# Attention blocks written to DRAM: GpSimd's DMA queue in place of SyncE's, for all head pairs but the last

## The chip, the cores and the metric

The kernel runs on one core of a Trainium2 chip. The metric is the device time of one execution in microseconds (us), from several executions of each kernel. A profiled execution gives, beside its own time, a trace of every engine: TensorE (PE, with its weight loads shown as PEld), VectorE (DVE), ScalarE (ACT), GpSimd (POOL) and SyncE (SP). DMAs are issued from the queues of SP, ACT and POOL; the issuing instructions stand in the trace as SPq, ACTq and, for GpSimd, as POOL rows named DMA_DIRECT2D.

## What is computed

One decoder layer for 512 tokens and 1024 channels in fp32, with two parallel attention branches of 8 heads of 64 channels each:

```
h = rms_norm(x, norm_w)
qa, ka, va, za, qb, kb, vb, zb, gl_a, gl_b = split(h @ w_in)
oa = moba_attention(rms_norm(qa), rms_norm(ka), va)       # softmax, with a bias by distance
ob = stick_breaking_attention(qb, kb, vb)                 # sigmoids and a running product along keys
ya = (oa * silu(za)) @ w_up_moba;  yb = (ob * silu(zb)) @ w_up_sb
x  = x + (sigmoid(gl_a + ba) * ya + sigmoid(gl_b + bb) * yb) @ w_out
```

With 512 tokens every past key is attended to in branch a, so each head has a lower-triangular matrix P of 512 x 512 weights, which is multiplied by its values. P is computed with queries on the partitions and is needed with keys on the partitions, so it has to be turned.

## The kernel before, in words

fp32 products run on TensorE as three passes over split operands: a high part `h` and a low part `l` (lines 234 to 236: l*h, h*l, h*h). Every weight block of 128 x 1024 comes in by one DMA from SP into a buffer `wr` (three buffers; line 160 in the stretch that matters here, line 179 elsewhere), ScalarE makes the high part `wh` (line 188), VectorE the low part `wl` (line 190). TensorE's first pass over a block needs only `wh`; its second needs `wl`. There are three buffers of each, so block n is loaded when `wl` of block n-3 is done, and split when TensorE is through with block n-3.

After the first products (up to about 145 us) comes a loop over eight pairs of heads, four of branch a (heads a0 to a7), then four of branch b (b0 to b7). For each pair:

- TensorE makes the scores of both heads (`scores`, line 513) into six PSUM banks, then multiplies the turned P of the pair two steps back by its values (`weighted`, line 608; `poa`, `pob`).
- VectorE and ScalarE make P row block by row block: in branch a (`softmax`, lines 533 to 541) with a bias tile `om` that SP loads by a DMA (`load_bias`, line 385; two buffers), in branch b (`stick`, lines 554 to 570) with scans on VectorE, in which `om` is written by ScalarE.
- `turn` (line 580) transposes P in blocks of 32 x 32 on VectorE into a tile `turned` (two buffers).
- `put` (line 587) writes `turned` to DRAM (`pd`) with four DMAs of 32 partitions, 160 KB each; `get` (line 594) reads it back in one DMA of 640 KB from ScalarE's queue into `pt`, with the 32 x 32 blocks in their turned places.
- Between these stand "fills": projections in chunks of 128 channels that have nothing to do with the pair (`gl`, `zb`, `kb`, and in later pairs `ya`, the product of branch a's output with its up-projection). They keep TensorE at work while P is made. The table `FILLS` says which fill stands where. `ya` of up:0 uses weight block 52, up:1 block 55.

GpSimd has little to do in the loop: at pairs 5, 6 and 7 it adds weight blocks in DRAM-to-SBUF DMAs for a later product (`sum_w`, lines 141 and 148). Each begins with a copy of one element that waits until the pair's `get` has landed, then loads a block, and then adds another onto it, once the first has landed.

The program's order on each engine is made by a scheduler that keeps data dependences and otherwise orders by its own estimates; the DMAs of one queue are issued in that order, and an instruction that waits holds what stands behind it on its engine or queue. ScalarE's queue too: a `get` that waits for its `put` holds ScalarE's next activation.

Of the kernel before, what the change touches and what calls it, by code (L numbers as in the profile page):

```python
# [32 lines left out]
PQ = 10 * 32  # L33
# [26 lines left out]
def hybrid_layer(ctx: ExitStack, tc: tile.TileContext, x, xT, w, rel, out):  # L60
    nc = tc.nc
# [232 lines left out]
    r = cp.tile([P, NT], F32, name="r")  # L294
# [288 lines left out]

    def put(br, h, turned):
        dr = dp.tile([P, 4 * PQ], F32, tag="pd", bufs=4, name=f"pd{br}{h}")
        for a in range(4):
            nc.sync.dma_start(bass.AP(tensor=dr.tensor, offset=dr.offset + a * PQ,
                                      ap=[[4 * PQ, 32], [32 * 4 * PQ, 4], [1, PQ]]),
                              turned[a * 32:(a + 1) * 32].rearrange("c q k r -> c q (k r)"))
        return dr  # L590

    def get(br, h, dr):
# [251 lines left out]
    for m, (br, p) in enumerate(PAIRS):  # L844
        raw[0] = br == "a"
        q, k = (qa, ka) if br == "a" else (qb, kb)
        sc = {h: {} for h in (2 * p, 2 * p + 1)}
        with tc.issue_after(end[0]):
            scores(br, p, q, k, sc)
        if m > 1:  # L850
            finish(m - 2, "pj")
        for b in range(2):
            h = 2 * p + b
            bias = load_bias(h) if br == "a" else None
            done[m, b] = put(br, h, turn(br, h, (softmax if br == "a" else stick)(h, sc[h], bias)))
            fill()
            if not b:
                done[m, 0] = get(*head(m, 0), done[m, 0])
        for b in range(2):
            if not b:  # L860
                done[m, 1] = get(*head(m, 1), done[m, 1])
            if (m, b) in SUMS:
                sum_w(SUMS[m, b], done[m, b])
            fill("pj" if (b or not fills[1]) and m < 7 else "s")
# [77 lines left out]
    for c in range(2):  # L942
        hi, lo = load_w()
        for t, ps, a, b in parts:
            for kk in range(2):
                k = 2 * c + kk
# [80 lines left out]
```

## Time and profile before

| | |
|---|---|
| three runs | 389.58, 388.64 and 423.43 us; median 389.58 |
| the profiled execution | 388.29 us, of which the span from first to last instruction is 386.5 |
| granted TensorE clock | 1.00 |
| busy share of the span | PE 98%, PEld 80%, DVE 74%, ACT 55%, POOL 21% |
| DMA | 86.38 MB, 223 GB/s |
| put's DMAs | 64 of 160 KB, all on SP; median 2.9 us (branch a) and 3.2 us (branch b) from issue to landing |

The one run of 423.43 us stands apart from the other two. The busy rows are of one execution; a wait is named by the engine and line that ended it last. In the timeline, a row's bracket is the idle time of the engine just before it.

### The profile page before, as it was taken

What the parts mean: (1) busy time and instruction counts of PE and PEld (TensorE: products, weight loads), DVE (VectorE), ACT (ScalarE), POOL (GpSimd) and SP (SyncE); (2) the same over time, 40 slices, a digit from 0 to 9 for tenths busy, and PEclk for the clock granted to TensorE, in tenths of its full rate; (3) what the DMA queues carried; (4) which work ended last, traced back from release to release, by engine and by line L of the source; (5) the groups of instructions that cost most, each with busy time, mean ns of one, the idle gap of its engine ahead of it and who ended that gap; (6) DMA issues with size and microseconds to landing.
All of it is one profiled execution on the core that took longest, in us unless ns stands there. A gap on an engine that the chain in (4) does not pass through costs nothing.

```text
span 386.5 us, 5481 instructions
## 1 busy us (share of the span) xinstructions
PE 379.2 (98%) x1935; PEld 308.3 (80%) x1935; DVE 284.5 (74%) x487; ACT 211.2 (55%) x367; POOL 80.0 (21%) x124
## 2 busy tenths in 40 slices
PE   8999999999999999999999999999999999999996
PEld 4888888888888998887878877776777877888885
DVE  4828999945777468972965399599939926999963
ACT  5685567338764447782853494554628213368540
POOL 3859959120210200000000000020101000420310
PEclk9999999999999999999999999999999999999999
DMA  7989799986864745569846826977697784599965
GB/s 264 342 332 336 198 234 274 283 277 238 209 173 100 190 124 187 146 204 335 242 110 207 308 69 213 303 181 226 190 332 257 159 331 132 173 254 294 177 155 175
DMA packets 36747, 86.38 MB, mean 223 GB/s; under 512 B 3944, under 2 KB 16744, under 8 KB 36720
## 3 DMA queue, kind: packets, MB, share of 16 engines
q1 hardware_dynamic: 27696, 52.72, 41.6%
q0 software_dynamic: 6576, 22.57, 24.6%
q10 hardware_dynamic: 2448, 10.75, 8.1%
q8 instruction: 15, 0.25, 0.2%
q14 instruction: 12, 0.10, 0.1%
HBM read 67.65 MB, written 14.70 MB: 213 GB/s over the span
## 4 chain that ended last, share of the span: by engine, by line
PE 82%; DVE 6%; DMA 5%; ACT 3%; issue 2%; SPq 2%; DVEq 0%
PE gl L234 6%; PE gl L235 6%; PE gl L236 6%; DMA pdb<-turnedb 3%; PE sa L513 2%; DMA wr<-in_w 2%; PE yb L234 2%; PE yb L235 2%; PE ka L235 2%; PE ka L234 2%; PE vx L235 2%; PE vx L234 2%; PE za L235 2%; PE za L234 2%; PE ka L236 2%; PE yb L236 2%
## 5 line engine op out<-in xcount | busy, mean ns | idle before, releaser
L190 DVE TENSOR_TENSOR wl<-wr,wh 128x1024 fp32r<-128x1024 f32 (+1 forms) x61 | 71.6, 1178 | 24.5 <-ACT wh L188 24.1
L188 ACT ACTIVATE wh<-wr 128x1024 fp32r<-128x1024 f32 (+1 forms) x61 | 63.2, 1036 | 46.2 <-DMA wr<-in_w 25.1
L234 PE MATMUL gl<-xl,wh 128*128 128x512 f32 x128 | 50.0, 391 | 0.0
L235 PE MATMUL gl<-xh,wl 128*128 128x512 f32 x128 | 49.8, 389 | 0.0
L236 PE MATMUL gl<-xh,wh 128*128 128x512 f32 x128 | 49.8, 389 | 0.0
L141 POOL COPY turn_of<-ptb 1x1 f32<-1x1 f32 x3 | 2.3, 758 | 148.9 <-DMA ptb<-pdb 148.9
L234 PEld LDWEIGHTS gl<-xl,wh 128*128 128x128 f32 x128 | 24.0, 188 | 5.2 <-issue 0.2
L236 PEld LDWEIGHTS gl<-xh,wh 128*128 128x128 f32 x128 | 24.0, 188 | 5.0
L235 PEld LDWEIGHTS gl<-xh,wl 128*128 128x128 f32 x128 | 24.0, 188 | 4.9
L635 ACT ACTIVATE gl<-gl,x 128x512 f32<-128x512 f32 x16 | 11.0, 685 | 20.8 <-PE gl L236 20.0
L533 DVE CUSTOM_DVE_ANT_0 pa<-sa,om 128x512 f32<-128x512 f32 (+3 forms) x32 | 13.9, 483 | 9.5 <-DMA om<-e_dr 6.8
L535 ACT ACTIVATE pa<-pa,m 128x512 f32<-128x512 f32 (+3 forms) x32 | 17.6, 552 | 5.0 <-DVE m L533 5.0
L558 DVE TENSOR_TENSOR_SCAN sx<-om,begin 128x512 f32<-128x512 f32 (+1 forms) x16 | 16.6, 1073 | 0.0
L580 DVE STREAM_TRANSPOSE turneda<-pa 128x384 f32<-128x384 f32 (+1 forms) x24 | 13.8, 605 | 2.6 <-ACT pa L539 2.4
L235 PE MATMUL ya<-oha,wl 128*128 128x512 f32 x32 | 12.8, 401 | 1.8 <-DVE wl L190 1.8
L580 DVE STREAM_TRANSPOSE turnedb<-pb 128x384 f32<-128x384 f32 (+1 forms) x24 | 13.6, 594 | 0.0
L234 PE MATMUL zb<-xl,wh 128*128 128x512 f32 x32 | 12.9, 404 | 0.0
L234 PE MATMUL kb<-xl,wh 128*128 128x512 f32 x32 | 12.7, 398 | 0.0
L234 PE MATMUL yb<-olb,wh 128*128 128x512 f32 x32 | 12.6, 393 | 0.0
L235 PE MATMUL zb<-xh,wl 128*128 128x512 f32 x32 | 12.5, 391 | 0.0
L236 PE MATMUL ya<-oha,wh 128*128 128x512 f32 x32 | 12.5, 390 | 0.0
L235 PE MATMUL yb<-ohb,wl 128*128 128x512 f32 x32 | 12.5, 390 | 0.0
(430 smaller groups left out, 1066.1 us busy)
## 6 DMA issues: line engine op xcount, KB each, us to landing
wr<-in_w SPq DMA_DIRECT2D x57, 512.0 KB, 5.5
pda<-turneda SPq DMA_DIRECT2D x32, 160.0 KB, 2.9
pta<-pda ACTq DMA_DIRECT2D x8, 640.0 KB, 5.1
pdb<-turnedb SPq DMA_DIRECT2D x32, 160.0 KB, 3.2
ptb<-pdb ACTq DMA_DIRECT2D x8, 640.0 KB, 4.9
qT<-in_w POOLq DMA_DIRECT2D x6, 512.0 KB, 5.9
xn<-in_x SPq DMA_DIRECT2D x8, 256.0 KB, 5.9
om<-e_dr SPq DMA_DIRECT2D x8, 256.0 KB, 4.3
```

The costliest lines, as they stand in the source:

```text
L141: with tc.issue_after(G.tensor_copy(turn_of, done[:1, :1].bitcast(F32)).ins):
L188: high[c] = A.activation(hi[:, a:b], raw[:, a:b], AF.Copy).ins
L190: low[c] = V.tensor_tensor(lo[:, a:b], raw[:, a:b], hi[:, a:b].bitcast(F32), op=ALU.subtract).ins
L234: T.matmul(ps, aH, bL, start=start, stop=False, skip_group_check=on)
L235: T.matmul(ps, aL, bH, start=False, stop=False, skip_group_check=on)
L236: end[0] = T.matmul(ps, aH, bH, start=False, stop=stop, skip_group_check=on).ins
L513: T.matmul(ps[b][:, c:c + n], x[o, i * P:(i + 1) * P], y[o, :n], start=m == 0, stop=m == 2)
L533: V.tensor_tensor_reduce(rows[i], sc[i], bias[:, S - n:], scale=1.0, scalar=3e38, op0=ALU.add, op1=ALU.min, accum_out=m[:, 0, i:i + 1])
L535: A.activation(rows[i], rows[i], AF.Exp, bias=m[:, 0, i:i + 1], scale=-1.0, accum_out=m[:, 1, i:i + 1])
L558: V.tensor_tensor_scan(sx[:, n - 1::-1] if n == S else sx[:, :n][:, ::-1], om[:, S + 1 - n:][:, ::-1], begin[:, S - n:S][:, ::-1], 0.0, op ...
L580: V.transpose(turned[:, :, at:at + n, :].rearrange("p q j r -> p j q r"), rows[i].rearrange("p (j q c) -> p j q c", j=n, q=4))
L635: evicted.append(A.activation(g, ps, AF.Identity if raw[0] else AF.Sigmoid, bias=mb[:, i:i + 1]).ins)
```

## The change

`put` takes its queue by the head: the last pair of branch b (heads b6 and b7) stays on SP, every other head's four DMAs are issued from GpSimd. Fourteen heads, 56 DMAs, move. What they copy, from where and to where, is the same.

```
     def put(br, h, turned):
         dr = dp.tile([P, 4 * PQ], F32, tag="pd", bufs=4, name=f"pd{br}{h}")
+        queue = nc.sync if br == "b" and h > 5 else nc.gpsimd
         for a in range(4):
-            nc.sync.dma_start(bass.AP(tensor=dr.tensor, offset=dr.offset + a * PQ,
-                                      ap=[[4 * PQ, 32], [32 * 4 * PQ, 4], [1, PQ]]),
-                              turned[a * 32:(a + 1) * 32].rearrange("c q k r -> c q (k r)"))
+            queue.dma_start(bass.AP(tensor=dr.tensor, offset=dr.offset + a * PQ,
+                                    ap=[[4 * PQ, 32], [32 * 4 * PQ, 4], [1, PQ]]),
+                            turned[a * 32:(a + 1) * 32].rearrange("c q k r -> c q (k r)"))
         return dr
```

From line 587 on, lines of the changed kernel have a number one higher. The scheduler also orders the other engines anew. Three places:

**The queues.** SP from head a4 to head b1, before (`wr` are weight blocks by their number, `om` bias tiles, `pda4` the DRAM block of head a4; x4 is four DMAs):

```order
L160 DMA wr46_2022<-in_w 128x1024
L587 DMA pda4_1915<-turneda4_1911 32x4x320 x4
L587 DMA pda5_1978<-turneda5_1974 32x4x320 x4
L587 DMA pda6_2121<-turneda6_2117 32x4x320 x4
L160 DMA wr47_2130<-in_w 128x1024
L385 DMA om1_121<-e_dr_88 128x512
L160 DMA wr48_2199<-in_w 128x1024
L160 DMA wr49_2234<-in_w 128x1024
L160 DMA wr50_2341<-in_w 128x1024
L587 DMA pda7_2190<-turneda7_2186 32x4x320 x4
L587 DMA pdb0_2332<-turnedb0_2328 32x4x320 x4
L587 DMA pdb1_2395<-turnedb1_2391 32x4x320 x4
```

and in the changed kernel:

```order
L160 DMA wr46_2022<-in_w 128x1024
L385 DMA om0_120<-e_dr_88 128x512
L385 DMA om1_121<-e_dr_88 128x512
L160 DMA wr47_2130<-in_w 128x1024
L160 DMA wr48_2199<-in_w 128x1024
L160 DMA wr49_2234<-in_w 128x1024
L160 DMA wr50_2341<-in_w 128x1024
L160 DMA wr51_2404<-in_w 128x1024
L160 DMA wr52_2439<-in_w 128x1024
```

Before, the bias tile of head a7 (`om1`) stands behind twelve puts, and blocks 51 and 52 behind those of a7, b0 and b1; now SP has only loads here. The puts stand on GpSimd, among the weight sums, in the changed kernel:

```order
L588 DMA pdb4_2762<-turnedb4_2758 32x4x320
L141 COPY turn_of_90<-ptb3_2650 1x1
L148 DMA T1b_2690<-in_w 128x1024
L588 DMA pdb4_2762<-turnedb4_2758 32x4x320
L148 DMA T1b_2690<-in_w 128x1024
L588 DMA pdb4_2762<-turnedb4_2758 32x4x320 x2
L588 DMA pdb5_2825<-turnedb5_2821 32x4x320 x4
```

Half of b4's put, and all of b5's, are behind the second T1b DMA, which adds onto the first and waits for its landing.

**VectorE ahead of `ya` of up:0**, before (`sx` and `pb` are the scans and P of a head, here of b2; `wl52` is the low part that `ya` waits for):

```order
L190 TENSOR_TENSOR wl51_2436<-wr51_2404,wh51_2435 128x1024
L558 SCALAR_TENSOR_TENSOR sx23_2532<-om1_121,begin_108 128x512
L558 SCALAR_TENSOR_TENSOR sx22_2537<-om0_120,begin_108 128x384
L560 TENSOR_TENSOR pb23_2528<-pb23_2528,sx23_2532 128x512
L560 TENSOR_TENSOR pb22_2529<-pb22_2529,sx22_2537 128x384
L568 SCALAR_TENSOR_TENSOR sx21_2542<-om_short_116,begin_108 128x386
L580 STREAM_TRANSPOSE turnedb2_2545<-pb23_2528 128x4x4x32
L570 TENSOR_TENSOR pb21_2527<-pb21_2527,sx21_2542 128x384
L580 STREAM_TRANSPOSE turnedb2_2545<-pb22_2529 128x3x4x32
L580 STREAM_TRANSPOSE turnedb2_2545<-pb21_2527 128x3x4x32
L190 TENSOR_TENSOR wl52_2555<-wr52_2439,wh52_2554 128x1024
```

and in the changed kernel:

```order
L190 TENSOR_TENSOR wl51_2436<-wr51_2404,wh51_2435 128x1024
L422 SCALAR_TENSOR_TENSOR kb3l_2467<-kb3_2441,kb3h_2466 128x512
L190 TENSOR_TENSOR wl52_2555<-wr52_2439,wh52_2554 128x1024
L558 SCALAR_TENSOR_TENSOR sx23_2532<-om1_121,begin_108 128x512
L558 SCALAR_TENSOR_TENSOR sx22_2537<-om0_120,begin_108 128x384
```

`wl52` has moved from behind all of b2's work to ahead of it.

**The pair of heads b4 and b5.** `wl55`, which `ya` of up:1 waits for, stands before behind the last transpose of b5; in the changed kernel it stands in the middle of b4:

```order
L781 TENSOR_TENSOR gl0_637<-ya0_2658,gl0_637 128x512
L781 TENSOR_TENSOR gl1_701<-ya1_2659,gl1_701 128x512
L558 SCALAR_TENSOR_TENSOR sx43_2745<-om1_121,begin_108 128x512
L560 TENSOR_TENSOR pb43_2741<-pb43_2741,sx43_2745 128x512
L558 SCALAR_TENSOR_TENSOR sx42_2750<-om0_120,begin_108 128x384
L580 STREAM_TRANSPOSE turnedb4_2758<-pb43_2741 128x4x4x32
L560 TENSOR_TENSOR pb42_2742<-pb42_2742,sx42_2750 128x384
L190 TENSOR_TENSOR wl55_2768<-wr55_2656,wh55_2767 128x1024
```

On TensorE, the last third of the scores of b4 and b5 (`sb41`, `sb51`) takes other PSUM banks. Before:

```order
L513 MATMUL sb52_2702<-kb2h_2157,qb2h_2161 128x384
L513 MATMUL sb41_2709<-kb2l_2158,qb2h_2161 128x256 [waits Activation_49]
L513 MATMUL sb41_2709<-kb2h_2157,qb2l_2162 128x256
L513 MATMUL sb41_2709<-kb2h_2157,qb2h_2161 128x256
L513 MATMUL sb41_2709<-kb2l_2158,qb2h_2161 128x128
L513 MATMUL sb41_2709<-kb2h_2157,qb2l_2162 128x128
L513 MATMUL sb51_2710<-kb2l_2158,qb2h_2161 128x256 [waits Activation_49]
```

and in the changed kernel:

```order
L513 MATMUL sb52_2702<-kb2h_2157,qb2h_2161 128x384
L513 MATMUL sb41_2709<-kb2l_2158,qb2h_2161 128x256 [waits DVE_49]
L513 MATMUL sb51_2710<-kb2l_2158,qb2h_2161 128x256 [waits DVE_49]
L513 MATMUL sb41_2709<-kb2h_2157,qb2l_2162 128x256
L513 MATMUL sb51_2710<-kb2h_2157,qb2l_2162 128x256
L513 MATMUL sb41_2709<-kb2h_2157,qb2h_2161 128x256
```

They waited for ScalarE to have read the scores of the same pair; now they wait for VectorE to have read `ya0` and `ya1` (`gl0`, `gl1` in the fence before, which stand right behind `wl53` and `wl54`). On ScalarE, the `get`s of b4 and b5 both stand ahead of the first activation of b6 before; in the changed kernel only that of b4 does.

## The prediction, as it went on record

> **What bounds the kernel now.** I read the page's busy shares first, then the windows of the pair loop, then what TensorE waited for, and last the queues and engines behind those waits.
>
> ```profile
> PE 379.2 (98%) x1935; PEld 308.3 (80%) x1935; DVE 284.5 (74%) x487; ACT 211.2 (55%) x367; POOL 80.0 (21%) x124
> ```
>
> TensorE is busy for 379.2 of 386.5 us at a granted clock of 1.00, and the change takes nothing off it. So it can win at most the part of the 7.3 idle us that the moved DMAs cause. The windows (us of the window, then busy us of PE, PEld, DVE, ACT, POOL, with instruction counts) say where in the loop there is any:
>
> ```profile
> 145.00:220.00 75.00, 75.00 (x412) 60.39 (x413) 48.85 (x135) 45.14 (x98) 0.00 (x0) 1.00 0.69 217
> 220.00:325.00 105.00, 102.51 (x558) 79.41 (x555) 82.54 (x120) 54.62 (x100) 6.39 (x9) 1.00 0.71 218
> ```
>
> Branch a's pairs leave none. From b0 on it is 105.00 - 102.51 = 2.5 us. The rest of the 7.3 lies at the start and in the tail, which the puts don't touch. TensorE's own timeline has the 2.5 us in three places:
>
> ```profile
> 256.70 0.50 PE L235 MATMUL ya<-oha,wl 128*128 128x512 f32 x1 [0.51 <-DVE wl L190]
> 264.05 0.38 PE L513 MATMUL sb<-kb2l,qb2h 64*128 64x256 f32 x1 [0.64 <-ACT pb L555]
> 280.71 0.50 PE L235 MATMUL ya<-oha,wl 128*128 128x512 f32 x1 [1.34 <-DVE wl L190]
> ```
>
> 0.51 + 0.64 + 1.34 = 2.49 us, all of it. Twice `ya` waits for the low part of its weight block (52, then 55); once the scores of b4 wait for a PSUM bank. SP's queue shows why the weight blocks are late (start, length from the first issue to the end of the last, count):
>
> ```profile
> 190.93 17.95 SPq L587 DMA_DIRECT2D pda<-turneda  x12
> 208.98 0.66 SPq L160 DMA_DIRECT2D wr<-in_w  x1
> 209.68 0.69 SPq L385 DMA_DIRECT2D om<-e_dr  x1
> ...
> 232.80 10.14 SPq L587 DMA_DIRECT2D pdb<-turnedb  x8
> 243.04 6.96 SPq L160 DMA_DIRECT2D wr<-in_w  x4
> ...
> L587 SPq DMA_DIRECT2D pdb<-turnedb x32: 303/432/1332, 232.8 to 307.9; - x32
> ```
>
> An issue takes 0.43 us (median), so the eight DMAs from 232.80 are 3.5 us of issuing in a stretch of 10.14. The rest is SP standing still for `turned`, with blocks 51 to 54 behind it until 243.04. And the bias tile of a7 goes out at 209.68, after twelve puts:
>
> ```profile
> 191.29 0.28 DVE L533 CUSTOM_DVE_ANT_0 pa<-sa,om 128x128 f32<-128x128 f32 x1
> 198.28 0.50 PE L513 MATMUL sa<-ka3l,qa3h 64*128 64x512 f32 x2
> 216.61 0.69 DVE L533 CUSTOM_DVE_ANT_0 pa<-sa,om 128x512 f32<-128x512 f32 x1 [6.26 <-DMA om<-e_dr]
> 219.20 0.50 PE L513 MATMUL sb<-kb0l,qb0h 64*128 64x512 f32 x2
> 224.26 1.28 ACT L554 ACT_TABLE_LOAD   x1
> 226.18 1.22 DVE L558 TENSOR_TENSOR_SCAN sx<-om,begin 128x512 f32<-128x512 f32 x1
> ```
>
> a7's scores exist from 198.28, its P is begun at 216.61. That pushes ScalarE's work on a7 to 224, so b0, whose scores begin at 219.20, gets its first scan at 226.18. **Branch b starts about 6 us late** and VectorE stays behind.
>
> **Part by part: what SP loses.** 56 issues of 0.43 us and their standing still go. The loads then wait for their buffers alone, that is for `wl` three blocks back. Of issuing alone 56 x 0.43 = 24 us leave SP; SP is on no path by itself, so this counts nothing.
>
> *The bias tile of a7* goes out ahead of the puts, right after that of a6. Its buffer was last read for a5, in the row at 191.29, so it is there when a7's scores are, and a6 and a7 are done one behind the other. I take it that ScalarE is through with a7 and its table loaded by 219, and b0's first scan comes 0.5 to 1 us after 219.20: at about 220 instead of 226.18, 6 us earlier.
>
> *Block 52.* Its load waits for nothing after 220, its `wh` for TensorE to be through with block 49. That is a `kb`, which ends where the scores of b2 begin:
>
> ```profile
> 240.19 0.50 PE L513 MATMUL sb<-kb1l,qb1h 64*128 64x512 f32 x2
> 261.91 0.50 PE L513 MATMUL sb<-kb2l,qb2h 64*128 64x512 f32 x2
> ...
> L190 DVE TENSOR_TENSOR wl<-wr,wh 128x1024 fp32r<-128x1024 f32 x27 | 32.3, 1206 | 2.8 <-ACT wh L188 2.7
> L188 ACT ACTIVATE wh<-wr 128x1024 fp32r<-128x1024 f32 x26 | 27.9, 1074 | 23.3 <-DMA wr<-in_w 21.8 <-issue 1.4
> ...
> 249.56 2.06 DVE L558 TENSOR_TENSOR_SCAN sx<-om,begin 128x512 f32<-128x512 f32 x2
> 255.47 1.18 DVE L190 TENSOR_TENSOR wl<-wr,wh 128x1024 fp32r<-128x1024 f32 x1
> 279.47 1.18 DVE L190 TENSOR_TENSOR wl<-wr,wh 128x1024 fp32r<-128x1024 f32 x1
> ```
>
> The split of `kb`, one `wh` and one `wl` later, 240.2 + 0.6 + 1.07 + 1.21, is 243.1, in the new order ahead of b2; needed at 256.2. Before, it began at 255.47. Term: **-0.51 us**, with 13 us to spare.
>
> *Block 55* was split at 279.47, behind b5. In the new order it stands behind two scans, two products and one transpose of b4, about 4 of the 5.9 us that a head of branch b takes on VectorE (255.47 - 249.56). b4's scores begin at 261.91 or a little before, and ScalarE and VectorE start on them 1 to 1.5 later, so `wl55` is done by about 268; needed at 278. Term: **-1.34 us**, with 10 us to spare.
>
> *The scores of b4 and b5* now wait for VectorE to have read `ya0` and `ya1`. By the new order, from b2's first scan at about 243.1 VectorE has two heads (11.8), three short operations of `kb`, `oa` and `ola` (1.9) and one of `zb` (0.6), so it is through with b3 at 257.4 (263.07 before), and with `wl53` and `wl54` at 259.8. `ya1` ends on TensorE with the fill, at 261.4 less the 0.51; its reading takes 0.6 to 0.7. TensorE comes to `sb51` 1.3 us after that fill ends. So the wait is 0 in the best case. In the worst, if VectorE were no earlier than before (263.07 + 2.4 + 1.3 = 266.8 against 262.6), it is 4.2. I take 0.3, since the 6 us of the late start decide and their cause is in the rows. Term: **-0.64 + 0.3 us**.
>
> **What GpSimd takes on.** No row has a put from GpSimd. The nearest are its loads of 128 rows, since a put is 128 pieces too:
>
> ```profile
> L444 POOL DMA_DIRECT2D kaT<-kadr x4: 536/537/538, 82.0 to 84.8; - x4
> L121 POOL DMA_DIRECT2D vT3a<-in_w x1: 1242/1242/1242, 48.7 to 48.7; - x1
> DMA to landing us min/median/max: 3.6/7.8/12.0
> ...
> 277.01 0.55 POOL L148 DMA_DIRECT2D T1b<-in_w  x1
> 283.42 0.86 POOL L148 DMA_DIRECT2D T1b<-in_w  x1 [5.85 <-DMA T1b<-in_w]
> ```
>
> From 0.54 to 1.24 us each: a put is 2.2 to 5.0 us of issue against 1.7 on SP. I take 2.2, the plain case of the same count of pieces. Heads come every 6 us or more, so the queue keeps up at either end. Cost on the path: nothing, as P is used two pairs later, about 20 us. The cover is thinnest where the second T1b DMA waits for the first, 6.4 us from 277.01 to 283.42, with half of b4's put behind it. T1b starts when b3's `get` lands. That `get` stands behind the first activation of b5 in the new order, at about 268 to 269, so T1b starts at about 274. The second T1b goes out at 280.4, and b4's put behind it is issued by 282 and lands by 287, at which b4's `get` lets ScalarE go on to b6. How late may that be? The rows of before have the landing times of branch b's puts and of its `get`s, the start of b6 on ScalarE, the `get`s of b6 and b7, and the last `pob`:
>
> ```profile
> DMA to landing us min/median/max: 2.1/3.2/6.5
> ptb<-pdb ACTq DMA_DIRECT2D x8, 640.0 KB, 4.9
> ...
> 291.94 0.58 ACT L554 ACTIVATE om<-sb 128x512 f32<-128x512 f32 x1
> 306.97 6.33 ACTq L594 DMA_DIRECT2D ptb<-pdb  x2
> 318.21 3.03 PE L608 MATMUL pob<-ptb,vbs 128*64 128x128 f32 x28
> ```
>
> The second of the two `get`s ends at 313.3 and lands 4.9 later, 26.3 us after b6's start. TensorE needs it for the second half of a run of 40 products from 318.21 less the gain, that is at 318.3. So b6 may begin at 292.0; 287 leaves 5 us.
>
> **The sum.** 388.29 - 0.51 - 1.34 - 0.34 = **386.1 us** for a profiled execution. The runs of before that agree, 388.64 and 389.58, have a mean of 389.1, 0.8 above their profiled one (their median of three, 389.58, is 1.3 above). So I predict **386.9 us** for the runs.
>
> One rule speaks against any gain. The Trainium skill (DMA: Bandwidth & Descriptors, Issuing engines are not separate DMA queues) says that DMAs of all issuing engines run on the same 16 DMA engines, and that issuing from more of them saves only sequencer time, usually small. By it the sum is -24 us of SP's time off the path, thus 388.3. The 10.14 us row disagrees: there the loads stood behind what the puts waited for, not behind their issue.
>
> Another (SBUF — State Buffer, Summary: rules for kernel authors) advises SP or ACT for a DMA under VectorE work, since GpSimd's descriptors starve while VectorE is in a doubled mode. These rows say which operations could be meant:
>
> ```profile
> L541 DVE TENSOR_SCALAR pa<-pa,m 128x256 f32<-128x256 f32 x8 | 2.8, 354 | 0.2
> L541 DVE TENSOR_SCALAR pa<-pa,m 128x128 f32<-128x128 f32 x8 | 2.3, 282 | 0.0
> ```
>
> 128 more elements in 72 ns is nearly two per ns, and they run in branch a alone. By that rule a put of branch a is up to 0.6 us late, where TensorE has no idle time; the three terms lie in branch b. So it doesn't raise the second rival below, as it would if all of VectorE's work shut GpSimd out.
>
> **The rivals.** *No gain:* the loads wait for their buffers nearly as long, or for the same DMA engines (busy share 0.71 in the loop), and the waits of `ya` stay. For: the 23.3 us that ScalarE idled before `wh` are mostly put down to the load itself. Against: buffers 52 and 55 come free over 10 us before they are needed. Time: 388.3 + 0.8 = 389.1.
>
> *VectorE's reading of `ya` becomes the wait.* If the start of branch b is less than about 4 us earlier, `sb51` waits up to 4.2 us where 0.64 was lost: -0.51 - 1.34 - 0.64 + 4.2 = +1.7, or 390.8. It decides as soon as b3's last transpose on VectorE ends after 259.0.
>
> *GpSimd's queue runs late.* At 1.24 us a DMA and 12.0 us to the landing of T1b, the second T1b goes out at 287.2, it and half a put are issued by 291.0, and it lands 3.2 to 6.5 later (median and slowest of these on SP), at up to 297.5: 5.5 us past the 292.0, all of them a wait of TensorE at the last `pob`. -2.2 + 5.5 = +3.3, or 392.4. It decides when b4's put lands after 292.
>
> That the change doesn't do what it says I leave out: the order has every put but two off SP.
>
> **How the numbers follow.** The forecast (a gain of 1.5 to 2.5 us) has 0.62, no gain 0.16, VectorE's reading 0.12, GpSimd's queue 0.10. The likeliest's own range is 386.0 to 388.2. Low end of the range: all 2.5 us gone, and runs that lie no higher than the profiled one less 0.5, 385.3. High end: the first slower rival, 390.8; past it lies half of the second. A measurement of this kernel can tell about 2%, 7.8 us, from no change. Faster by that has 0.01, since TensorE's idle time in reach is 2.5 us; slower by that 0.04, for a queue that is later than both bounds; within it 0.95.
>
> **What would show it.** Right: `om` of a7 issued before 200 and no wait of VectorE for it; b0's first scan near 220; no wait of `ya` for `wl`; GpSimd's put DMAs near 0.54 us; PE busy in 220 to 325 but for some 0.3 us. Wrong: PE waiting for `gl` at the scores of b4 or b6, for a `ptb` at `pob`, or b4's put landing after 292. If GpSimd's DMAs take over 1.24 us each, or ScalarE stands at `get`s of branch a, the bounds above are too narrow.

## The result, and the profile after

The changed kernel is slower: median 391.1 us of 20 runs, beside 388.75 of the kernel before; ratio 1.0053, 95% interval 1.0033 to 1.0073. Four of the changed kernel's runs (395.5 to 396.05 us) and one of the kernel before (423.43) lie apart from the others, and the ratio leaves them out. The difference is within 2%, on the wrong side of the forecast of 386.9 and just past its range (385.3 to 390.8). The profiled execution took 391.13 us, span 389.3 (before 388.29 and 386.5).

The same two windows as before (us, then busy us of PE, PEld, DVE, ACT, POOL), and what TensorE waited for in the loop:

```profile
145.00:220.00 75.00, 75.00 (x413) 60.41 (x413) 52.09 (x143) 49.48 (x109) 17.69 (x32) 1.00 0.73 239
220.00:325.00 105.00, 100.44 (x548) 78.20 (x546) 79.52 (x111) 50.35 (x89) 18.31 (x33) 0.98 0.67 208
```
```profile
PE gl L234 <- DVE ob L614: 3.4, 1, 3.4
PE kb L234 <- DVE zb L623: 1.1, 1, 1.1
```

The three old waits (`ya` twice, the scores of b4) are gone. Two new ones stand in the loop, 3.4 and 1.1 us, and the granted clock, 1.00 before, is 0.98. TensorE's timeline at the larger one:

```profile
293.23 0.39 PE L236 MATMUL zb<-xh,wh 128*128 128x512 f32 x1
297.06 0.47 PE L234 MATMUL gl<-xl,wh 128*128 128x512 f32 x1 [3.44 <-DVE ob L614]
297.36 0.40 PE L235 MATMUL gl<-xh,wl 128*128 128x512 f32 x1
...
299.13 0.63 PE L235 MATMUL gl<-xh,wl 128*128 128x512 f32 x1
299.56 0.63 PE L236 MATMUL gl<-xh,wh 128*128 128x512 f32 x1
299.99 0.63 PE L234 MATMUL gl<-xl,wh 128*128 128x512 f32 x1
```
```profile
298.50:301.70 3.20, 3.20 (x9) 2.43 (x9) 3.20 (x5) 0.50 (x1) 0.02 (x1) 0.50 0.82 262
```

The wait is for a PSUM bank of `pj`, which VectorE frees by reading `pob1` into `ob1` (line 614). Behind it eight matmuls start 0.43 us apart instead of 0.23: the clock is 0.50 there, and 8 x 0.2 = 1.6 us more are lost. Backwards from it, GpSimd, ScalarE and VectorE:

```profile
273.61 0.55 POOL L588 DMA_DIRECT2D pdb<-turnedb  x1 [10.73 <-DVE turnedb L580]
...
274.38 0.56 POOL L148 DMA_DIRECT2D T1b<-in_w  x1
275.25 0.56 POOL L588 DMA_DIRECT2D pdb<-turnedb  x1 [0.32 <-issue]
278.99 0.91 POOL L148 DMA_DIRECT2D T1b<-in_w  x1 [3.19 <-DMA T1b<-in_w]
279.57 3.10 POOL L588 DMA_DIRECT2D pdb<-turnedb  x5
```
```profile
279.71 1.66 ACT L643 ACTIVATE gl<-gl 128x512 f32<-128x512 f32 x3
288.45 0.33 ACTq L595 DMA_DIRECT2D ptb<-pdb  x1
288.83 0.60 ACT L554 ACTIVATE om<-sb 128x512 f32<-128x512 f32 x1 [7.46 <-DMA pdb<-turnedb]
```
```profile
289.46 1.23 DVE L558 TENSOR_TENSOR_SCAN sx<-om,begin 128x512 f32<-128x512 f32 x1 [5.15 <-ACT om L554]
...
295.79 0.51 DVE L570 TENSOR_TENSOR pb<-pb,sx 128x384 f32<-128x384 f32 x1
296.23 0.68 DVE L614 TENSOR_TENSOR ob<-pob,zb 128x512 f32<-128x512 f32 x1
```

Half of b4's put stands behind the second T1b DMA, which waits for the first. The put goes out by about 280.7 and lands at 288.45, where b4's `get` leaves ScalarE; ScalarE has stood idle for 7.46 us by then, some 4 of them after b6's first scores were there. So b6's first scan is at 289.46, though b6's scores were begun at 283.51, and `ob1`, ready soon after 288, is read behind eight operations of b6 and one `wl`. Where TensorE stands along the loop (starts of the scores of b2, b4, b6 and of the last `pob`; before: 240.19, 261.91, 286.19, 318.21):

```profile
241.61 0.50 PE L513 MATMUL sb<-kb1l,qb1h 64*128 64x512 f32 x2
262.53 0.50 PE L513 MATMUL sb<-kb2l,qb2h 64*128 64x512 f32 x2
283.51 0.50 PE L513 MATMUL sb<-kb3l,qb3h 64*128 64x512 f32 x2
...
320.64 4.54 PE L609 MATMUL pob<-ptb,vbs 128*64 128x128 f32 x40
```

It is 2.7 us ahead at b6's scores and 2.4 behind at the last `pob`: 5.1 us lost in this one place, 3.6 from start to start and 1.6 of half rate.

### The profile page after: what moved, and what is told of

Same layout as the page of the kernel before. It is cut to its first block, busy times and chain, and to the rows that moved or that the text cites. A ratio compares the mean times of both kernels' runs of the same rounds, so it can differ in the third digit from the quotient of the medians.

```text
span 389.3 us, 5495 instructions
## 1 busy us (share of the span) xinstructions
PE 379.9 (98%) x1935; PEld 309.0 (79%) x1935; DVE 285.1 (73%) x487; ACT 211.1 (54%) x367; POOL 109.0 (28%) x180
## 4 chain that ended last, share of the span: by engine, by line
PE 84%; DVE 5%; issue 4%; DMA 3%; POOL 1%; ACT 1%; DVEq 0%; ACTq 0%; POOLq 0%
PE gl L234 7%; PE gl L236 7%; PE gl L235 7%; PE sa L513 2%; PE kb L234 2%; PE yb L234 2%; PE kb L236 2%; PE ka L235 2%; PE ka L236 2%; PE yb L236 2%; PE kb L235 2%; PE yb L235 2%; PE vx L236 2%; PE vx L235 2%; PE za L236 2%
## 5 line engine op out<-in xcount | busy, mean ns | idle before, releaser
L234 PE MATMUL gl<-xl,wh 128*128 128x512 f32 x128 | 50.8, 397 | 3.4 <-DVE ob L614 3.4
L588 POOL DMA_DIRECT2D pda<-turneda x32 | 17.7, 555 | 63.7 <-DVE m L536 42.5
L588 POOL DMA_DIRECT2D pdb<-turnedb x24 | 14.0, 660 | 39.6 <-DVE turnedb L580 35.6
L554 ACT ACTIVATE om<-sb 128x512 f32<-128x512 f32 (+1 forms) x16 | 8.9, 558 | 13.4 <-DMA pdb<-turnedb 7.5
L329 POOL TENSOR_SCALAR e_sb<-rb 8x1 f32<-8x1 f32 (+11 forms) x32 | 10.7, 362 | 6.5 <-DMA rb<-in_rel 6.5
```

The source lines that it names most:

```text
L234: T.matmul(ps, aH, bL, start=start, stop=False, skip_group_check=on)
L329: last["table"] = G.tensor_scalar(e_sb[:, m:m + n], rb[:, b:b + 1].to_broadcast([H, n]), -1.0, 1.0, op0=ALU.mult, op1=ALU.mult).ins
L588: queue.dma_start(bass.AP(tensor=dr.tensor, offset=dr.offset + a * PQ, ap=[[4 * PQ, 32], [32 * 4 * PQ, 4], [1, PQ]]), turned[a * 32:(a + 1 ...
```

## The experiments

Medians are of one group of runs on one chip beside the kernel before (388.6 to 388.9 in the four groups). "Half rate" counts the runs with a mean granted clock below 0.997; in a run without a trace the clock is all that is known, not what TensorE waited for.

**b4's and b5's puts back on SyncE.**
```
-        queue = nc.sync if br == "b" and h > 5 else nc.gpsimd
+        queue = nc.sync if br == "b" and h > 3 else nc.gpsimd
```


> Only the puts of b4 and b5 go back to SyncE; VectorE's order around `ob1` stays nearly as in the changed kernel (`ob1` behind b6's scans). Theory 1 (b4's put stands behind T1b's sum in GpSimd's queue, so its `get` holds ScalarE to 288.45, b6's scans start at 289.46 instead of about 285.0, and `ob1`, which stands seven operations behind the first of them, frees a bank of `pj` 3.4 us too late): b4's `get` goes out before 280, `ob1` is read by 291.5, no wait of `gl` (3.4 us gone), no half-rate stretch behind it (1.6 us gone, granted clock 1.00), the wait of `kb` of 1.1 us stays: 391.1 - 3.4 - 1.6 = 386.1, bounds 385.6 to 387.0. Theory 2 (VectorE's new order alone makes the wait, whenever the put lands): `gl` still waits at least 2 us, 389 or more. Theory 3 (GpSimd's puts cost by themselves, through the DMA engines, all along): 48 of 56 puts are still there, 390.5.

387.1 us, ratio 0.9941 (0.9919 to 0.9964), no wait of `gl`, half rate in none of 12 runs. Theory 1's step holds. Theories 2 and 3 fall: `ob1` still stands behind b6's scans, and 48 of 56 puts are still on GpSimd. The median is 1 us above the 386.1, mostly in the spread from 386.3 to 387.9.

**VectorE reads `pob1` first.**
```
+        last["po"] = V.tensor_tensor(dst, po..., z, op=ALU.mult).ins
-            with tc.issue_after(split_of[1]) if h % 2 == 0 and i == 3 else nullcontext():
+            with tc.issue_after(last["po"] if h == 6 else split_of[1]) if h % 2 == 0 and i == 3 else nullcontext():
```


> All of the changed kernel's puts stay on GpSimd; VectorE's reading of `pob1` is put ahead of b6's first scan. Theory 1: b4's `get` is as late as before (288.4), b6's first scan is at 289.5, but `ob1` is read at about 288 to 290, so the 3.4 us wait of `gl` and the 1.6 us of half rate are gone, 1.1 us of `kb` stay: 386.1, bounds 385.6 to 387.2. Theory 2 says the same here. Theory 3 (late puts cost by themselves, wherever VectorE reads): the wait moves to another place, `pob` or `ya`, and the time stays at 389 or more.

A miss for theory 1: 390.63 us, ratio 1.0039 (1.0012 to 1.0067), half rate in 9 of 12. The `gl` wait is gone and another has come. What TensorE waited for, and VectorE's timeline:

```profile
PE ya L235 <- DVE wl L190: 2.5, 1, 2.5
```
```profile
291.68 1.23 DVE L190 TENSOR_TENSOR wl<-wr,wh 128x1024 fp32r<-128x1024 f32 x1 [7.02 <-ACT wh L188]
292.82 0.68 DVE L614 TENSOR_TENSOR ob<-pob,zb 128x512 f32<-128x512 f32 x1
293.42 2.06 DVE L558 TENSOR_TENSOR_SCAN sx<-om,begin 128x512 f32<-128x512 f32 x2
...
306.39 2.31 DVE L190 TENSOR_TENSOR wl<-wr,wh 128x1024 fp32r<-128x1024 f32 x2
```

b4's `get` leaves ScalarE at 288.48 as in the changed kernel, so b6 is late all the same. Its first scan, 293.42, is where the kernel before had it (293.02), while TensorE comes over 2 us earlier; the next thing behind b7 on VectorE, `wl` of block 59, makes TensorE wait for what it had won. So the place of `ob1` only says where the late put is paid. I took that order for a part of the cause, and it isn't.

**The sum of T1b one pair later.**
```
-SUMS = {(4, 1): ("T1a",), (5, 1): ("T1b",), (6, 1): ("T2a",)}
+SUMS = {(4, 1): ("T1a",), (6, 1): ("T1b", "T2a")}
```


> All puts stay on GpSimd; the sum of T1b is made one pair later, together with T2a, so that no sum stands ahead of b4's put. Theory 1: b4's put lands by 279, no wait of `gl`, 386.1, bounds 385.6 to 387.5 (two sums at once at about 300 share the DMA engines with the last `get`s). Theory 2: `gl` waits 2 us or more, 389 or more. Theory 3: 390.5.

386.92 us, ratio 0.9944 (0.992 to 0.9968), half rate in none of 12: all puts on GpSimd, and a gain. The two sums at once cost 0.7 us at the last `pob`, which waited for its load.

**Only branch a's puts on GpSimd.**
```
+        queue = nc.sync if br == "b" else nc.gpsimd
```


> Only branch a's puts are on GpSimd, all of branch b's are on SyncE as before; VectorE's order is nearly that of the changed kernel, with `ob1` even further back, behind b7's first scan. Theory 1: the bias tile of a7 is early as in the changed kernel, so is b0's first scan (222.9), no sum stands ahead of a put, `ob1` is read by about 293, so `gl` waits 0 to 0.5 us, and the loads of blocks 52 and 55 stand ahead of the puts of their pairs, so `ya` does not wait: 386.3, bounds 385.6 to 387.5. Theory 2: the wait of `gl` is 3 us or more, 389.5. If the loads of the weights still stood behind branch b's puts, `ya` would wait up to 1.9 us again: 388.

385.48 us, ratio 0.9894 (0.9857 to 0.9932), 0.8 below theory 1's 386.3. One wait is left in the loop, `kb` for `zb`, 1.1 us.

**The same, and `zb0` earlier on VectorE.**
```
+        last["z"] = V.tensor_tensor(zr[br, p], ps, zr[br, p], op=ALU.mult).ins
+        with tc.issue_after(last["z"]) if h == 1 else nullcontext():
             V.tensor_tensor_scan(sx[:, :n][:, ::-1], short...
```


> The kernel with only branch a's puts on GpSimd (385.5 us), and VectorE's product of `zb0` put ahead of b1's last scan, so that the bank of `pj` for `kb3` comes free earlier. If the one wait left in its loop (`kb` for `zb`, 1.1 us at about 236) is VectorE's order alone: `zb0` is read at about 232.5 instead of 235.2, the wait is gone, nothing takes its place: 384.4, bounds 384.0 to 384.9. If VectorE is simply full there, `kb` no longer waits but b1 and b2 are later by as much and a `ya` waits instead: 385.5.

385.27 us, ratio 0.9913 (0.9893 to 0.9933): the wait falls from 1.1 to 0.4 (`zb0` is read at 234.60), but the runs lie between 384.6 and 386.3, and the two medians don't tell whether the time fell.

**b4's put alone, of branch b's, on GpSimd.**
```
+        queue = nc.gpsimd if br == "a" or h == 4 else nc.sync
```


> The kernel with only branch a's puts on GpSimd (385.5 us), and b4's put alone on GpSimd as well: four DMAs more, in the one place where they stand behind the sum of T1b. The theory after the first four runs (one late put, that of b4, holds ScalarE at its `get` to about 288.5 and with it b6 and b7 on VectorE; TensorE falls back to the timetable of before at whatever stands behind them, `gl` or `ya`): a wait of 2.5 to 3.5 us at 293 to 308, in part of the runs 1.7 us of half rate behind it: 388 without the half rate, 389.7 with it, median 389.3, bounds 387.8 to 390.5. If it takes many puts on GpSimd (traffic or descriptor work all along), four DMAs change nothing: 385.7.

A miss: 385.79 us, ratio 0.9913 (0.9893 to 0.9932). GpSimd's timeline, and ScalarE's:

```profile
273.83 0.55 POOL L148 DMA_DIRECT2D T1b<-in_w  x1 [0.48 <-ACT pb L555]
276.02 0.57 POOL L588 DMA_DIRECT2D pdb<-turnedb  x1 [1.64 <-DVE turnedb L580]
277.88 0.89 POOL L148 DMA_DIRECT2D T1b<-in_w  x1 [1.29 <-DMA T1b<-in_w]
278.48 1.99 POOL L588 DMA_DIRECT2D pdb<-turnedb  x3
```
```profile
284.73 0.33 ACTq L595 DMA_DIRECT2D ptb<-pdb  x1
285.89 0.60 ACT L554 ACTIVATE om<-sb 128x512 f32<-128x512 f32 x1 [3.14 <-PE sb L513]
```

The put is issued by 280.5, no sooner than in the changed kernel, yet lands 4.3 us later instead of 7.7, just as b6's scores arrive. One of its six runs took 391.73 at a clock of 0.991; what it waited for was not recorded.

**Only the bias tiles off SyncE** (the kernel before, all puts on SyncE).
```
     def load_bias(h):
-        nc.sync.dma_start(bt, ...
+        nc.gpsimd.dma_start(bt, ...
```


> The kernel before, all puts on SyncE, and only the bias tiles of a2 to a7 (six loads) go through GpSimd's queue. If the late bias tile of a7 behind the puts is what makes branch b late, and with it the weight blocks and the scores that TensorE waits for: b0's first scan at about 223 instead of 226.2, the waits of `ya` and `sb` gone but for some 0.5 us, 386.6, bounds 385.8 to 387.4. If the weight loads behind branch b's own puts are a cause of their own, the two waits of `ya` stay, 0.5 + 1.3: 388.3. If neither matters, 388.9.

386.74 us, ratio 0.9946 (0.9928 to 0.9964). The edit moves all eight bias loads, not six: those of a0 and a1 go out at 27.7 us, long before the loop, the other six from 153.0 to 185.8. b0's first scan is at 223.71, and the window of the loop has no idle time:

```profile
220.00:325.00 105.00, 105.00 (x579) 82.43 (x578) 81.79 (x113) 52.01 (x90) 6.29 (x9) 1.00 0.73 227
```

With branch b in time all three old waits are gone, and branch b's own puts ahead of the weight loads cost nothing. The time is near that of the kernels with 48 or 56 moved puts in which nothing waits for b4's (386.0 to 387.1), and above the 385.48 of the one with branch a's 32. Its profile has a wait of TensorE of 1.5 us near the start (`psR`), outside the loop, that the others don't have; what brings that on was not tested.

**Only branch b's puts on GpSimd.**
```
+        queue = nc.sync if br == "a" or h > 5 else nc.gpsimd
```


> Only branch b's puts (b0 to b5) are on GpSimd, branch a's on SyncE. Theory: a7's bias tile is late as in the kernel before, b0's first scan at about 226, and b4's put stands behind the sum of T1b and lands at 290 or later; the waits of `ya` for blocks 52 and 55 are gone (1.9 us), but b6 is late and `gl` or `ya` waits 3 us or more: 390, bounds 388.5 to 392.5. If taking branch b's puts off SyncE were a gain by itself, 387.0.

391.93 us, ratio 1.009 (1.0066 to 1.0113), half rate in all six. b0's first scan is at 226.24, as late as before, and yet the waits of `ya` for block 52 and of b4's scores are gone: from b2's scores to b4's TensorE took 20.92 us (240.26 to 261.18), as in the changed kernel, where it had taken 21.72 before. So branch b in time is enough to remove these two waits, but not needed: taking branch b's puts off SyncE does it too. The mechanism came a pair earlier than expected, with b2's put in the sum of T1a. ScalarE at b2's `get`, and TensorE:

```profile
268.43 0.33 ACTq L595 DMA_DIRECT2D ptb<-pdb  x1
268.80 0.60 ACT L554 ACTIVATE om<-sb 128x512 f32<-128x512 f32 x1 [11.89 <-DMA pdb<-turnedb]
```
```profile
272.22 0.79 PE L234 MATMUL zb<-xl,wh 128*128 128x512 f32 x1 [6.59 <-ACT gl L636]
```

**b4's load issued by SyncE.**
```
-        nc.scalar.dma_start(pt, dr)
+        (nc.sync if br == "b" and h == 4 else nc.scalar).dma_start(pt, dr)
```


> The changed kernel with one DMA moved: the load of b4's P (`ptb4`) is issued by SyncE instead of ScalarE, so that ScalarE doesn't stand in front of it; the put of b4 stays on GpSimd behind the sum of T1b and is as late as in the changed kernel. If ScalarE standing at that load is the step by which the late put reaches TensorE: b6's first activation starts at about 284.5, `ob1` is read by 292, no wait of `gl`, no half rate, 1.1 us of `kb` stay: 386.3, bounds 385.6 to 387.2. If the late put reaches TensorE another way (the DMA engines, `pob`): 389 or more.

387.46 us, ratio 0.9964 (0.9943 to 0.9985), from 385.4 to 390.6: mostly the first case, with a median just above its bounds. The profiled run is the slowest of the 12 and shows a second way. Here b4's put landed later than in the changed kernel (its load goes out at 292.80), and b6's first activation is at 284.68, but VectorE:

```profile
287.93 1.13 DVE L560 TENSOR_TENSOR pb<-pb,sx 128x512 f32<-128x512 f32 x2
292.65 0.71 DVE L580 STREAM_TRANSPOSE turnedb<-pb 128x512 f32<-128x512 f32 x1 [3.58 <-DMA pdb<-turnedb]
```

b6's transpose writes the buffer of `turned` that b4's put still reads. So a late put has two holders: ScalarE at the `get`, VectorE at the buffer.

**b5's put alone back on SyncE.**
```
+        queue = nc.sync if br == "b" and h > 4 else nc.gpsimd
```


> The changed kernel with b5's put alone back on SyncE; b4's put stays on GpSimd behind the sum of T1b. With b4's put alone on GpSimd in branch b there was no wait: its last DMA went out at 280 as in the changed kernel, but landed 4 to 5 us later instead of 8, and SyncE's weight loads stood behind b5's put until 284.5. If it is the weight loads, free to go at 280 to 288 in the changed kernel, that fill the DMA engines beside the sum and the put: here they stand behind b5's put again, b4's load goes out at about 285, no wait, 386.5, bounds 385.8 to 387.3. If the place behind the sum decides alone, the load goes out at 288 and `gl` waits 3 us: 389 to 391.

391.64 us, ratio 1.008 (1.0057 to 1.0104), half rate in 5 of 6; the profiled run is the sixth, with a wait of `gl` of 1.9 us. b4's load goes out at 288.29, as in the second case. The first is not wholly excluded: the weight loads went out at 281.9 and 284.1 here, later than in the changed kernel (280.3 and 281.4), but not as late as with b4's put alone (284.5 and 285.0).

**`ob1` read late, with no put on GpSimd** (the kernel before; the product that reads `pob1` is kept in `held` until b6's last transpose).
```
+            if held:
+                with tc.issue_after(last["turn"]):
+                    held.pop()()
```


> The kernel before, all puts on SyncE; VectorE's reading of `pob1` is held back behind b6's last transpose, so that TensorE waits for the bank of `pj` with no put on GpSimd. Expected wait: `ob1` is read at about 299.6 instead of 290.7, `gl` was due at about 296.1, 3 to 3.6 us. If TensorE's own idle time of 3 us brings the half rate behind it: a stretch with 0.427 us between matmuls instead of 0.227 in some or all runs, 388.7 + 3.3 + 1.7 = 393.7 with it, 392.0 without. If the half rate comes of GpSimd's DMAs or the DMA engines' load instead: granted clock 1.00 in all runs, 392.0.

391.03 us, ratio 1.0057 (1.0029 to 1.0086). The wait is 1.8 us, half of what I had worked out. Four of 8 runs have a clock of 1.00 (388.8 to 390.3), four 0.994 to 0.996 (391.8 to 393.8). The profiled one:

```profile
298.59 0.52 PE L234 MATMUL gl<-xl,wh 128*128 128x512 f32 x1 [1.82 <-DVE ob L613]
```
```profile
299.00:302.30 3.30, 3.30 (x9) 2.56 (x8) 3.30 (x5) 0.69 (x2) 0.86 (x1) 0.50 0.98 216
```

So the half rate comes behind TensorE's idle time without any put on GpSimd.

**The same DMAs on the same queues, T1b's sum behind b4's put.**
```
-SUMS = {(4, 1): ("T1a",), (5, 1): ("T1b",), (6, 1): ("T2a",)}
+SUMS = {(4, 1): ("T1a",), (6, 1): ("T2a",)}
+            if (m, b) == (6, 0):
+                with tc.issue_after(last["put"]):
+                    sum_w(("T1b",), done[5, 1])
```


> The changed kernel with the same DMAs on the same queues, and one order turned round on GpSimd: the sum of T1b is issued behind b4's put instead of into it (so three of b5's four DMAs now stand behind it). If the place of b4's put behind the sum is the cause: b4's put is issued by 275.5 and lands by about 279, its load stands in no one's way, no wait of `gl`, no half rate, 1.1 us of `kb` stay: 386.3, bounds 385.6 to 387.4. If the traffic of the sum in that stretch is the cause, whatever the order: b4's load goes out at 286 or later, `gl` waits, 389 to 391. If b5's put, now late itself, takes its place (its buffer of `turned` is b7's, its load stands on ScalarE): a wait of VectorE for it at 293 to 297, and 388.

386.01 us, ratio 0.994 (0.9918 to 0.9962), half rate in none of 6, one wait in the loop (`kb`, 1.1). GpSimd and ScalarE:

```profile
273.77 2.24 POOL L588 DMA_DIRECT2D pdb<-turnedb  x4 [11.41 <-DVE turnedb L580]
...
276.52 0.56 POOL L148 DMA_DIRECT2D T1b<-in_w  x1 [0.28 <-issue]
279.73 0.56 POOL L588 DMA_DIRECT2D pdb<-turnedb  x1 [2.65 <-DVE turnedb L580]
280.71 0.91 POOL L148 DMA_DIRECT2D T1b<-in_w  x1 [0.43 <-DMA T1b<-in_w]
```
```profile
279.02 0.33 ACTq L595 DMA_DIRECT2D ptb<-pdb  x1
```

This settles that the place behind the sum is the cause. With nothing taken off GpSimd or off the DMA engines, the `get` goes out 9.4 us earlier (279.02 instead of 288.45) and the time falls by 5.1 us. Half of the 9.4 is the earlier issue (the put has gone out by 276.0, not 280.7), the other half the landing, 3.0 us after the last issue instead of 7.7. The three DMAs of b5's put that now stand behind the sum landed after 10.3 to 10.9 us, and b5's `get` went out at 293.47; TensorE waited for none of it.

## Why the prediction was wrong, step by step

*The bias tile of a7: right, over-sized.* Its load goes out by 186.3 instead of 209.68. b0's first scan is at 222.94, 3.2 us earlier, not 6:

```profile
219.37 0.69 ACT L636 ACTIVATE gl<-gl,x 128x512 f32<-128x512 f32 x1 [3.80 <-PE gl L236]
219.95 1.05 ACT L188 ACTIVATE wh<-wr 128x1024 fp32r<-128x1024 f32 x1
221.02 1.28 ACT L554 ACT_TABLE_LOAD   x1
222.32 0.60 ACT L554 ACTIVATE om<-sb 128x512 f32<-128x512 f32 x1
```

I took the table as loaded by 219. It is loaded with b0's first Sigmoid, behind the eviction of a fill and a `wh`. The kernel with only the bias tiles moved shows that 2.5 us are enough for the three old waits.

*Blocks 52 and 55, the scores of b4: right, under-sized.* All three waits are gone, the 0.3 too. I priced them by the idle time of the matmuls, 2.49. From b2's scores to b6's TensorE took 46.00 us before and 41.90 now: 4.1. The waits of the weight loads in the kernel before had said so, 3.0 + 1.0:

```profile
PEld ya L235 <- DVE wl L190: 3.0, 3, 1.8
PEld sb L513 <- ACT pb L555: 1.0, 1, 1.0
```

*The wait of `kb`, 1.1 us: missed.* The earlier b1 stands ahead of `zb0` on VectorE, and `zb0` holds the bank that `kb3` needs. I had counted VectorE's time for `zb`, not who waits for its bank.

*GpSimd's price per DMA: right.* 0.55 us median, 0.54 taken.

*The step that failed* is "Cost on the path: nothing", with its margin: "So b6 may begin at 292.0; 287 leaves 5 us." The landing was near (288.45 for 287), though in two parts that offset each other: the put was out by 280.7 instead of 282, and took 7.7 us to land instead of 5. The limit was wrong. I asked only when the last `pob` needs b6, and took the start of b6 on ScalarE in the kernel before as the time that it may have. b6 began 3.1 us earlier than there, at 288.83, and TensorE waited, because it was itself 2.7 us earlier and because VectorE does TensorE's work behind b6: `ob1` here, `wl` of block 59 in the second experiment. In six of the seven kernels whose profiled run waited 1.1 us or less in the loop, b4's `get` went out at 279.0 to 280.6, three or more us ahead of b6's scores; in the seventh, with b4's put alone, at 284.73, as they came. So the limit was between 284.7 and 288.3, not 292.0.

*The rivals.* "GpSimd's queue runs late" (0.10) named the right kind of cause, a late put on GpSimd, at the wrong place and by the wrong steps (its DMAs took 0.55 us, not 1.24, and the first T1b DMA landed in 4.2 us, not 12.0), with a point of decision (a landing after 292) over 3 us too late. "VectorE's reading of `ya`" gave nearly the measured time, but `ya` was read in time; the number is chance. "No gain" did not come about as argued: the old waits did go, and a new one took more than they gave. The rule of the Trainium skill (DMA: Bandwidth & Descriptors, Issuing engines are not separate DMA queues) that was set beside it, that another issuing engine saves sequencer time alone, does not agree with the moved bias tiles, 2.0 us faster. What a queue's order cost here was the standing behind another DMA's wait, not the issue.

*The half rate: not thought of.* In the profiled run 1.6 us more were lost behind the 3.4 us wait. Five of the changed kernel's 20 runs have a clock of 1.000 and lie at 388.7 to 389.6, the others at 390.3 and more. Without the half rate the change would probably have come out near no change; how long the five waited was not recorded.

*Open:* why b4's put, issued to its end behind the sum by 280.5 to 282.4, landed 4.3 us later in one kernel and 6.5 to 10.4 us later in four others (weight loads that go out earlier are not shown to be it: with b5's put ahead of them on SyncE it still took 6.5); and the spread of about 1 us between runs of one kernel where no wait differs.

## What to carry to other kernels

A DMA that is moved to a quieter queue inherits the waits of that queue: look for what waits there and ask which half of the moved DMAs stands behind it. The limit for lateness comes from every engine's order behind the late work, on the new timetable: a gain ahead of that place shortens the margin by as much. Where one small DMA stands behind the others and is waited for, it can be enough to move that one: the bias loads alone took away the same three waits as 48 puts.

## What the runs showed of the hardware

**Half rate after a short wait.** In the profiled runs, waits of TensorE of 1.8, 3.3 and 3.4 us were each followed by a stretch of 3.4 us at a granted clock of 0.50, with matmuls of 512 columns 0.43 us apart; with a wait of 6.6 us the stretch was 6.8 us and began inside the wait (0.72 from 270.0 to 272.2). Waits of 1.9 and 2.5 us in two other profiled runs were followed by none, so a wait of this size can bring it and need not. Counted by the clock, it is in 15 of the changed kernel's 20 runs, in 9 of 12 with `pob1` read first, in 6 of 6 with only branch b's puts, in 5 of 6 with b5's put back on SyncE, in 4 of 8 with `ob1` read late and in 1 of 12 with b4's load on SyncE. In the seven kernels whose profiled run waited 1.1 us or less in the loop it is in 1 of 54 runs (the one of 391.73 us), and in the kernel before, with waits of up to 1.3 us, in 1 of 72. The Trainium skill (TensorE: Matmul & The Clock Gate, Part 1: The HAM clock gate) gives half rate after an idle window of about 3.4 us. The rate agrees with these runs; the idle time that brings it on can be shorter here, 1.8 us.

**Idle time read from matmul rows is too small.** A matmul's row is 0.39 us long where the next begins after 0.23, so each wait shows shorter than it is, 3.44 for 3.83 from start to start (3.60 more than the usual 0.23).

**Most puts behind an accumulating DMA landed late.** In the changed kernel the two put DMAs issued ahead of the second T1b DMA landed in 2.5 and 3.8 us, the four issued from 279 to 281.5, behind it, in 7.2 to 8.7. In the kernel with the order turned round the five ahead of it took 2.5 to 5.8 us, the three behind it 10.3 to 10.9. With b4's put alone the three behind it took about 5. Why is open.
